# A seventh tile of columns in the first projection stage, with wider weight rows and one bank for two modulation sums

## The chip, the core and the metric

The kernel runs on one core of a Trainium2 chip. Five engines work beside one another: TensorE (PE in the profile; its weight loads are listed as PEld) multiplies matrices into PSUM, VectorE (DVE) and ScalarE (ACT) do elementwise work, GpSimd (POOL) clears a few tiles, and SyncE (SP) issues all DMAs, one after the other, in the order of its queue. The metric is the device time of one execution in microseconds.

## What is computed

One layer of a diffusion backbone: 256 latent tokens and 256 context tokens of width 2048. Everything starts with a modulated RMS norm and one wide projection; its columns feed an RWKV-7 branch (r, k, v, decay and rate inputs wd and ad, gate z), a latent-attention branch (q, kv, rope key, gate) and merge gates.

```python
def modulation(cond, w_mod, b_mod):
    m = (jax.nn.silu(cond) @ w_mod + b_mod).reshape(-1, 1, 3 * D_MODEL)
    return jnp.split(m, 3, axis=-1)

def project_stream(h, norm_w, shift, scale, w_in):
    hm = rmsnorm(h, norm_w) * (1 + scale) + shift
    return split_in(hm @ w_in)

...
        (rkv_x, zr_x, wd_x, ad_x, qd_x, kvd_x, kr_x, zm_x, mg_x) = project_stream(x, norm_w[i], sh_x, sc_x, w_in[i])
        (rkv_c, zr_c, wd_c, ad_c, qd_c, kvd_c, kr_c, zm_c, mg_c) = project_stream(ctx, norm_w[i], sh_c, sc_c, w_in[i])
...
        _, y_x = rwkv_scan(r_x, v_x, kk_x, dec_x, a_x, km_x, S_ctx)
...
        att_x = blocked_attend(q_x, jnp.concatenate([k_x, k_c], axis=1),
                               jnp.concatenate([v_x_att, v_c_att], axis=1))
        o_ml_x = att_x * jax.nn.silu(zm_x)

        x_new = x + g_x * merge_branches(o_rw_x, o_ml_x, mg_x, w_branch_rwkv[i], w_branch_mla[i], w_out[i])
```

The columns at issue are `kvd`, the 256 inputs of the keys and values of attention. They are needed for both streams, so a tile of 128 of these columns is 512 tokens wide.

## The kernel before

**Number format.** A product in full precision is three matmuls of rounded halves (`mm3`, line 234): high by high, high by low, low by high. A weight piece is loaded, cast to its high half on ACT (`wh`) and its low half is formed on DVE (`wl`); both are in `split` and `parts_of`, and profile lines show them as line 122, since a helper records every elementwise operation; matmuls show line 103, transposes line 107. The tiles are told apart by their names.

**First stage** (lines 256 to 389). The tokens `xT` lie transposed in 16 blocks of 128 rows, k = 0 to 15. For each k the modulation needs shift and scale of 128 channels: `mod_a(k)` loads four 512 KB pieces `wm` of the modulation's weights (11 buffers), multiplies them by `ssil`, the SiLU of the conditions, into a PSUM bank `pm` (32 matmul instructions), and copies the partial sums to `part`. `mod_b(k)` transposes `part` into the other half of the same bank and adds up on DVE, which gives `mod`. `scale_x`, two ACT operations and a split then make the modulated block, `hmh[:, k]` and `hml[:, k]`. `first(k, half)` multiplies it by the weights `w_first[k]`, 768 columns in two pieces of 384, three tiles of 128 columns per half, and adds into six accumulators `a0` to `a5` of 512 tokens. These are wd, ad, and k and v of the first two pairs of heads.

The loop of line 357 is written out as a software pipeline, and PE, ACT and DVE keep the order of the code: in turn k stand the modulated block k, `first(k-1, 0)`, `mod_a(k+1)`, `scale_x(k+1)`, the splits of the weights of k, `first(k-1, 1)`, `mod_b(k+1)`. SP's order is the planner's: the trace shows w_first(k), then the four wm of k+1. The two pieces of `w_first` take buffers of the general weight tag `w`, of which there are four; a `wl` of a half has two buffers, so its next one waits for `first` of the turn before.

Ahead of the loop stand the sums of squares of `xT`, `mod_a(0)`, `mod_b(0)`, the reciprocal root `rms`, and a matmul with the diagonal `dg` that spreads it over the partitions (`pst`, copied to `rsb`). On SP the order is vectors, constants, `xT` (4 MB in four), `cond`, then weights.

**PSUM** has eight banks in four tags of two: `acc`, `wk`, `lv`, `ch`. In the first stage the six accumulators hold `acc`, `wk`, `lv`, and the `pm` of even and odd k hold `ch`. Later `ch` carries the state updates of the scan (`chp`), `acc` the projections, `wk` the small work of the chains.

**Behind it.** Behind the first stage three things run together: a front chain that prepares heads, a back chain that scans them, and a background of projection tiles, `bg`. A background tile (`proj_g`) is 48 matmuls of 256 tokens, or of 512 where both streams are needed, with four weight pieces of 256 KB; it is taken in steps between the steps of the chains, and a clock of modelled engine times decides while tracing how many steps go where. The background takes what the chains need first (`main`), else the next of `extra`: the two kv tiles, 24 merge gates, the rope key, four q tiles, eight attention gates, eight merge gates. `kv_g(i)` projects tile 76 + i and spills it to DRAM, with sums of squares (`spill`). During attention the background gets a fixed number of steps per round (line 1401); what is left, the last merge gates and 16 tiles of the first branch's output (`branch_g`), runs in a row at line 1420, and then come the second branch and the output projection.

Of the kernel before, what the change touches and what calls it, by code (L numbers as in the profile page):

```python
# [9 lines left out]
F32 = mybir.dt.float32  # L10
# [3 lines left out]
ALU = mybir.AluOpType  # L14
AX = mybir.AxisListType

P = 128
D = 2048
KT = D // P
T = 256  # L20
TT = 2 * T
# [105 lines left out]
def hybrid_block(  # L127
# [20 lines left out]
    nc = tc.nc  # L148
# [65 lines left out]
    def piece(src, shape, pool=None):  # L214

        w = (pool or place[0]).tile(shape, F32, name="w", tag="w", bufs=NWU if pool else place[1])
        nc.sync.dma_start(w, src)
        return w

    def parts_of(w, pool=None, ns=None):  # L220

        h = (pool or place[0]).tile(list(w.shape), F32R, name="wh", tag="wh", bufs=ns or place[2])
        l = (pool or place[0]).tile(list(w.shape), F32R, name="wl", tag="wl", bufs=ns or place[3])
        with tc.high_priority(HP):
            split(w, h, l)
        return h, l
# [27 lines left out]
    lrl = cvp.tile([P, 2, TT], F32R, name="lrl", bufs=1)  # L254
    pp = ctx.enter_context(tc.tile_pool(name="pp", bufs=2, space=PSUM))
    with tc.tile_pool(name="p1", bufs=2) as p1:
        xT = p1.tile([P, KT, TT], F32, name="xT", bufs=1)
        for q in range(4):
            nc.sync.dma_start(xT[:, 4 * q:4 * q + 4], xcT[:, 4 * q:4 * q + 4])

        cv2 = p1.tile([P, 32], F32, name="cv2", bufs=1)
        nc.sync.dma_start(cv2, cond)
        st = p1.tile([P, 32], F32, name="st", bufs=1)
        S.activation(st, cv2, AF.Tanh, scale=0.5)
        V.scalar_tensor_tensor(st, st, 1.0, cv2, ALU.add, ALU.mult)
        V.memset(ssil, 0.0)
        V.tensor_scalar(ssil[:, 0:2 * KT], st, 0.5, None, ALU.mult)

        parts, mods = {}, {}

        def load_mod(k):
            for r in range(4):
                wm = p1.tile([P, 4, 256], F32, name="wm", tag="wm", bufs=NWM)
                nc.sync.dma_start(wm, w_mod_ss[k][:, 4 * r:4 * r + 4])
                yield wm

        def mod_a(k):

            pm = pp.tile([P, 512], F32, name="pm", tag="ch")
            for r, wm in enumerate(load_mod(k)):  # L280
                for g in range(4):
                    k0 = 2 * (4 * r + g)
                    E.matmul(pm[32 * g:32 * g + 32, 0:256], lhsT=ssil[:, k0:k0 + 32], rhs=wm[:, g],
                             start=r == 0, stop=r == 3, tile_position=(0, 32 * g))
            part = p1.tile([P, 256], F32, name="part", tag="part")
            S.copy(part, pm[:, 0:256])
            parts[k] = pm, part

        def mod_b(k):

            pm, part = parts.pop(k)
            for i in range(2):
                E.transpose(pm[:, 256 + 128 * i:384 + 128 * i], part[:, 128 * i:128 * i + 128], ident)
            mod = p1.tile([P, 4], F32, name="mod", tag="mod", bufs=4)
            for i in range(2):
                V.tensor_reduce(mod[:, 2 * i:2 * i + 2],
                                pm[:, 256 + 128 * i:384 + 128 * i].rearrange("p (g c) -> p c g", c=32)[:, 0:2], AX.X, ALU.add)
            V.tensor_scalar(mod[:, 0:2], mod[:, 0:2], vec("bsh", k), None, ALU.add)
            V.tensor_scalar(mod[:, 2:4], mod[:, 2:4], vec("bsc", k), 1.0, ALU.add, ALU.add)
            V.tensor_scalar(mod[:, 2:4], mod[:, 2:4], vec("norm", k), None, ALU.mult)  # L300
            mods[k] = mod


        pst = pp.tile([P, TT], F32, name="pst", tag="wk")
        for k in range(KT):
            sq = p1.tile([P, TT], F32, name="sq", tag="sq", bufs=4)
            if k % 2:
                S.activation(sq, xT[:, k], AF.Square)
            else:
                V.tensor_tensor(sq, xT[:, k], xT[:, k], ALU.mult)  # L310
            g = k % 4
            E.matmul(pst[32 * g:32 * g + 32], lhsT=con("ones")[:, 0:32], rhs=sq, start=k < 4, stop=k >= KT - 4,
                     tile_position=(0, 32 * g))
        sqs = p1.tile([P, TT], F32, name="sqs", tag="sq", bufs=4)
        S.copy(sqs, pst)
        pst = pp.tile([P, TT], F32, name="pst", tag="wk")
        for i in range(4):
            E.matmul(pst[:, 2 * i:2 * i + 2], lhsT=sqs[:, 128 * i:128 * i + 128], rhs=con("ones")[:, 0:2], start=True, stop=True)
        mod_a(0)
        mod_b(0)  # L320
        ms = p1.tile([P, 8], F32, name="ms", bufs=1)
        V.tensor_scalar(ms, pst[:, 0:8], 1.0 / (32 * D), 1e-6, ALU.mult, ALU.add)
        rms = p1.tile([P, 8], F32, name="rms", bufs=1)
        rsqrt(p1, rms, ms, 8)
        pst = pp.tile([P, TT], F32, name="pst", tag="lv")
        dg = p1.tile([P, 4, P], F32, name="dg", bufs=1)
        V.tensor_tensor(dg, ident.unsqueeze(1).to_broadcast([P, 4, P]), rms[:, 0:8:2].unsqueeze(2).to_broadcast([P, 4, P]), ALU.mult)
        E.matmul(pst, lhsT=con("ones"), rhs=dg.rearrange("p i t -> p (i t)"), start=True, stop=True)
        rsb = p1.tile([P, TT], F32, name="rsb", bufs=1)
        S.copy(rsb, pst)  # L330

        acc = [pp.tile([P, TT], F32, name=f"a{i}", tag=("acc", "wk", "lv")[i // 2]) for i in range(6)]
        wks = {}

        def first(k, half):
            wh, wl = wks[k][half]
            for i in range(3 * half, 3 * half + 3):
                cs = slice(128 * (i % 3), 128 * (i % 3) + 128)
                mm3(acc[i], wh[:, cs], wl[:, cs], hmh[:, k], hml[:, k], k == 0, k == KT - 1)

        hxs, ws = {}, {}

        def load_first(k):
            ws[k] = [piece(w_first[k][:, 384 * i:384 * i + 384], [P, 384]) for i in range(2)]

        def split_first(k):
            wks[k] = [parts_of(w) for w in ws.pop(k)]

        def scale_x(k):
            hxs[k] = p1.tile([P, TT], F32, name="hx", tag="hx")  # L350
            V.tensor_tensor(hxs[k], xT[:, k], rsb, ALU.mult)

        with tc.manual_schedule(engines={mybir.EngineType.PE, mybir.EngineType.Activation, mybir.EngineType.DVE}):
            scale_x(0)
            for k in range(KT + 1):
                if k < KT:
                    load_first(k)
                    mod, hx = mods.pop(k), hxs.pop(k)  # L360
                    for i in range(2):
                        t0 = slice(T * i, T * i + T)
                        S.activation(hx[:, t0], hx[:, t0], AF.Identity, scale=mod[:, 2 + i:3 + i], bias=mod[:, i:i + 1])
                    split(hx, hmh[:, k], hml[:, k])
                if k > 0:
                    first(k - 1, 0)
                if k + 1 < KT:
                    mod_a(k + 1)
                    scale_x(k + 1)
                if k < KT:  # L370
                    split_first(k)
                if k > 0:
                    first(k - 1, 1)
                if k + 1 < KT:
                    mod_b(k + 1)
        wd = p1.tile([P, TT], F32, name="sq", tag="sq", bufs=4)
        S.activation(wd, acc[0], AF.Tanh)
        split(wd, lrh[:, 0], lrl[:, 0])
        split(acc[1], lrh[:, 1], lrl[:, 1])

        def conv_kv(p, k, v):
            ck = cvp.tile([P, TT], F32, name="ck", tag="ck")
            conv(ck, k, "ck", p, 2)
            cv = cvp.tile([P, TT], F32, name="cv", tag="cv")
            conv(cv, v, "cv", p, 2)
            ckv[p] = (ck, cv)

        conv_kv(0, *acc[2:4])
        conv_kv(1, *acc[4:6])
# [96 lines left out]
        V.tensor_copy(sqd[:, col:col + 4], pss[:, 0:4])  # L486

    def kv_g(i):
        ps = yield from proj_g(76 + i, TT)
        for j in range(2):  # L490
            yield from spill(kvd[:, i, T * j:T * j + T], ps[:, T * j:T * j + T], 8 * i + 4 * j)

# [1012 lines left out]
def _layout(i):  # L1505
# [36 lines left out]
    wr, wk, wv = w[:, :1024], w[:, 1024:2048], w[:, 2048:3072]  # L1542
    wzr, wwd, wad, wqd = w[:, o[1]:o[2]], w[:, o[2]:o[3]], w[:, o[3]:o[4]], w[:, o[4]:o[5]]
    wkv, wkr, wzm, wmg = w[:, o[5]:o[6]], w[:, o[6]:o[7]], w[:, o[7]:o[8]], w[:, o[8]:o[9]]
    first = np.concatenate([wwd, wad, wk[:, :128], wv[:, :128], wk[:, 128:256], wv[:, 128:256]], 1)
    a["w_first"] = ca(first.reshape(KT, P, 768))
    allp = np.concatenate([wr, wzr, wzm, wk, wv, wmg, wqd, wkv], 1)
    nt = allp.shape[1] // P
    a["w_proj"] = ca(allp.reshape(2, 8, P, nt, P).transpose(3, 0, 2, 1, 4).reshape(nt, 2, P, 1024))
# [35 lines left out]
```

## Time and profile before

| | us |
|---|---|
| runs before: 1301.01, 1299.57, 1303.21; median | 1301.01 |
| profiled execution, first to last instruction (span) | 1295.7 |
| median less span | 5.3 |
| last matmul of the first stage ends, about | 135.7 |
| last branch store of the scan issued (orwd) | 912.7 |
| drain of the background starts | 1090.0 |

The list of runs has no time of its own for the profiled execution; its span is the time against which sums are made. In the views, a group is named by line, engine, operation and out<-in; a bracket at the end of a line gives the idle time of the engine before it and what ended it. The chain that ended last is followed back from the last instruction, at each step to what released it or to the one before it on its engine.

### The profile page before, as it was taken

What the parts mean: (1) busy time and instruction counts of PE and PEld (TensorE: products, weight loads), DVE (VectorE), ACT (ScalarE), POOL (GpSimd) and SP (SyncE); (2) the same over time, 40 slices, a digit from 0 to 9 for tenths busy, and PEclk for the clock granted to TensorE, in tenths of its full rate; (3) what the DMA queues carried; (4) which work ended last, traced back from release to release, by engine and by line L of the source; (5) the groups of instructions that cost most, each with busy time, mean ns of one, the idle gap of its engine ahead of it and who ended that gap; (6) DMA issues with size and microseconds to landing.
All of it is one profiled execution on the core that took longest, in us unless ns stands there. A gap on an engine that the chain in (4) does not pass through costs nothing.

```text
span 1295.7 us, 30060 instructions
## 1 busy us (share of the span) xinstructions
PE 1238.3 (96%) x11484; PEld 1040.8 (80%) x11484; DVE 949.4 (73%) x2658; ACT 571.1 (44%) x1183; POOL 3.3 (0%) x9
## 2 busy tenths in 40 slices
PE   5999989999999999999999998999999999999998
PEld 2666878788878778877788887878888889999887
DVE  4444876868797788788978886866877777569655
ACT  3343542442443433524524344343566655445443
POOL 0000000000000000000000000000000000000000
PEclk9999999989999999999999999999999999999999
DMA  9998445544453434533533445432853325988684
GB/s 375 356 358 308 126 136 143 140 127 113 107 143 100 118 97 121 141 79 104 154 99 103 113 121 131 114 97 88 247 169 113 102 59 168 309 273 278 214 264 140
DMA packets 172319, 212.09 MB, mean 164 GB/s; under 512 B 68560, under 2 KB 96848, under 8 KB 171664
## 3 DMA queue, kind: packets, MB, share of 16 engines
q1 hardware_dynamic: 172176, 210.18, 53.3%
q8 instruction: 90, 1.47, 0.5%
q14 instruction: 53, 0.43, 0.1%
HBM read 195.30 MB, written 14.82 MB: 162 GB/s over the span
## 4 chain that ended last, share of the span: by engine, by line
PE 66%; DVE 15%; DMA 13%; ACT 3%; issue 2%; SPq 1%; DVEq 0%; ACTq 0%
PE acc L103 31%; PE chp L103 11%; PE lv L103 9%; PE wk L103 6%; DMA w<-in_w_proj 5%; DMA wm<-in_w_mod_ss 4%; PE a L103 4%; DVE wl L122 4%; PE ch L103 3%; DVE BK L122 2%; PE wk L107 2%; ACT wh L122 1%; DVE wt L122 1%; PE pm L103 1%; DMA xT<-in_xcT 1%
## 5 line engine op out<-in xcount | busy, mean ns | idle before, releaser
L122 ACT CAST wh<-w 128x512 fp32r<-128x512 f32 (+1 forms) x484 | 291.4, 607 | 360.3 <-PE acc L103 144.2
L122 DVE TENSOR_TENSOR wl<-w,wh 128x512 fp32r<-128x512 f32 (+1 forms) x480 | 322.4, 675 | 146.9 <-ACT wh L122 89.4
L103 PE MATMUL acc<-hmh,wh 128*128 128x256 f32 (+1 forms) x1328 | 422.8, 319 | 4.4 <-ACT wh L122 4.2
L103 PE MATMUL acc<-hmh,wl 128*128 128x256 f32 (+1 forms) x1312 | 402.1, 307 | 4.9 <-DVE wl L122 4.7
L103 PE MATMUL acc<-hml,wh 128*128 128x256 f32 (+2 forms) x1328 | 406.1, 306 | 0.0
L103 PEld LDWEIGHTS acc<-hmh,wh 128*128 128x128 f32 x1328 | 252.2, 190 | 30.2 <-issue 7.4
L103 PEld LDWEIGHTS acc<-hmh,wl 128*128 128x128 f32 x1312 | 248.9, 190 | 22.1 <-DVE wl L122 8.3
L103 PEld LDWEIGHTS acc<-hml,wh 128*128 128x128 f32 (+1 forms) x1328 | 251.6, 189 | 11.4 <-issue 0.7
L122 DVE TENSOR_TENSOR pr<-wt 64x14 f32<-64x14 f32 (+6 forms) x224 | 42.6, 190 | 2.8
L122 DVE TENSOR_TENSOR wt<-wt,pr 64x14 f32<-64x14 f32 (+6 forms) x224 | 42.2, 189 | 2.3
L103 PE MATMUL a<-hmh,wh 128*128 128x512 f32 x96 | 40.7, 424 | 0.0
L122 DVE TENSOR_TENSOR W<-WT,lv 128x512 f32<-128x512 f32 x48 | 32.9, 685 | 9.8 <-PE lv L103 9.3
L103 PE MATMUL pm<-wm,ssil 128*32 128x256 f32 x512 | 34.9, 385 | 4.8 <-DMA wm<-in_w_mod_ss 4.5
L103 PE MATMUL a<-hmh,wl 128*128 128x512 f32 x96 | 37.9, 395 | 0.4 <-DVE wl L122 0.4
L103 PE MATMUL a<-hml,wh 128*128 128x512 f32 x96 | 37.9, 395 | 0.0
L103 PE MATMUL chp<-obh,wh 128*128 128x256 f32 x128 | 36.2, 283 | 0.0
L103 PE MATMUL chp<-obl,wh 128*128 128x256 f32 x128 | 36.2, 283 | 0.0
L103 PE MATMUL chp<-obh,wl 128*128 128x256 f32 x128 | 36.2, 283 | 0.0
L103 PEld LDWEIGHTS lv<-W,Z 64*64 64x64 f32 x1024 | 31.3, 135 | 3.6 <-issue 1.2
L122 ACT ACTIVATE hx<-hx,mod 128x256 f32<-128x256 f32 x32 | 17.5, 594 | 37.8 <-DVE mod L122 37.8
L122 DVE TENSOR_TENSOR AQ<-wk,cc 128x256 f32<-128x256 f32 (+1 forms) x48 | 24.4, 509 | 13.1 <-PE wk L103 12.7
L103 PE MATMUL lv<-W,Z 64*64 64x64 f32 x1024 | 33.8, 220 | 0.0
(314 smaller groups left out, 2107.6 us busy)
## 6 DMA issues: line engine op xcount, KB each, us to landing
w<-in_w_proj SPq DMA_DIRECT2D x296, 256.0 KB, 3.1
wm<-in_w_mod_ss SPq DMA_DIRECT2D x64, 512.0 KB, 7.5
w<-in_w_mod_g SPq DMA_DIRECT2D x64, 256.0 KB, 3.5
w<-in_w_br SPq DMA_DIRECT2D x64, 256.0 KB, 4.1
w<-in_w_out SPq DMA_DIRECT2D x64, 256.0 KB, 3.3
w<-in_w_first SPq DMA_DIRECT2D x32, 192.0 KB, 5.0
thd<-th SPq DMA_DIRECT2D x48, 128.0 KB, 3.5
xT<-in_xcT SPq DMA_DIRECT2D x4, 1024.0 KB, 8.5
```

The lines of the kernel that those rows point to most:

```text
L103: return self.engine.matmul(out, lhsT=lhsT, rhs=rhs, **kw)
L107: return self.engine.transpose(*a)
L122: return fn(out, *a, **kw)
```

## The change

- `cond` is loaded ahead of `xT`.
- One PSUM tile `pmm` in `ch` is allocated for the whole stage. The modulation of even k uses its first 256 columns, that of odd k the second 256; the transposes of `mod_b` go into the columns that `mod_a` had used for the same k.
- `mod_b(0)` is moved behind the matmul with `dg`.
- The freed `ch` bank holds a seventh accumulator `a6`: the first 128 columns of kv.
- `w_first[k]` has 896 columns, loaded in one DMA with rows of 3.5 KB into a tag `wf` of its own with two buffers, and split as 512 + 384 columns. `first` takes four tiles in its first half and three in its second.
- `kv_g(0)` no longer projects; it spills `a6`.

```diff
     with tc.tile_pool(name="p1", bufs=2) as p1:
+        cv2 = p1.tile([P, 32], F32, name="cv2", bufs=1)
+        nc.sync.dma_start(cv2, cond)
         xT = p1.tile([P, KT, TT], F32, name="xT", bufs=1)
...
-        cv2 = p1.tile([P, 32], F32, name="cv2", bufs=1)
-        nc.sync.dma_start(cv2, cond)
...
+        pmm = pp.tile([P, 512], F32, name="pm", tag="ch")
...
-            pm = pp.tile([P, 512], F32, name="pm", tag="ch")
+            pm = pmm[:, 256 * (k % 2):256 * (k % 2) + 256]
...
-                    E.matmul(pm[32 * g:32 * g + 32, 0:256], lhsT=ssil[:, k0:k0 + 32], rhs=wm[:, g],
+                    E.matmul(pm[32 * g:32 * g + 32], lhsT=ssil[:, k0:k0 + 32], rhs=wm[:, g],
...
-                E.transpose(pm[:, 256 + 128 * i:384 + 128 * i], part[:, 128 * i:128 * i + 128], ident)
+                E.transpose(pm[:, 128 * i:128 * i + 128], part[:, 128 * i:128 * i + 128], ident)
...
         mod_a(0)
-        mod_b(0)
...
+        mod_b(0)
         S.copy(rsb, pst)
 
-        acc = [pp.tile([P, TT], F32, name=f"a{i}", tag=("acc", "wk", "lv")[i // 2]) for i in range(6)]
+        acc = [pp.tile([P, TT], F32, name=f"a{i}", tag=("acc", "wk", "lv", "ch")[i // 2]) for i in range(7)]
...
-            for i in range(3 * half, 3 * half + 3):
-                cs = slice(128 * (i % 3), 128 * (i % 3) + 128)
+            for i in range(4 * half, 4 + 3 * half):
+                cs = slice(128 * (i % 4), 128 * (i % 4) + 128)
...
-            ws[k] = [piece(w_first[k][:, 384 * i:384 * i + 384], [P, 384]) for i in range(2)]
+            ws[k] = p1.tile([P, 896], F32, name="wf", tag="wf", bufs=2)
+            nc.sync.dma_start(ws[k], w_first[k])
...
-            wks[k] = [parts_of(w) for w in ws.pop(k)]
+            w = ws.pop(k)
+            wks[k] = [parts_of(w[:, 0:512]), parts_of(w[:, 512:896])]
...
-        ps = yield from proj_g(76 + i, TT)
+        ps = (yield from proj_g(77, TT)) if i else acc[6]
...
-    first = np.concatenate([wwd, wad, wk[:, :128], wv[:, :128], wk[:, 128:256], wv[:, 128:256]], 1)
-    a["w_first"] = ca(first.reshape(KT, P, 768))
+    first = np.concatenate([wwd, wad, wk[:, :128], wv[:, :128], wk[:, 128:256], wv[:, 128:256], wkv[:, :128]], 1)
+    a["w_first"] = ca(first.reshape(KT, P, 896))
```

## What the change does to the time: the prediction

> **What bounds the kernel now.** First the page: its head, the engines' totals and the 40 slices.
>
> ```profile
> span 1295.7 us, 30060 instructions
> PE 1238.3 (96%) x11484; PEld 1040.8 (80%) x11484; DVE 949.4 (73%) x2658; ACT 571.1 (44%) x1183; POOL 3.3 (0%) x9
> ...
> DMA  9998445544453434533533445432853325988684
> GB/s 375 356 358 308 126 136 143 140 127 113 107 143 100 118 97 121 141 79 104 154 99 103 113 121 131 114 97 88 247 169 113 102 59 168 309 273 278 214 264 140
> ```
>
> TensorE (PE) is busy nearly everywhere, but in the first four slices of 32.4 us the DMA engines are full as well. That is the first stage, the one that is edited. So the second view is the table of stretches, and the third the chain that ended last, cut to the first stage.
>
> ```profile
> 28.00:34.00 6.00, 4.71 (x39) 2.28 (x42) 3.75 (x11) 2.30 (x5) 0.00 (x0) 1.00 1.03 399
> 34.35:124.71 90.36, 86.64 (x680) 55.82 (x676) 40.44 (x117) 37.85 (x78) 0.00 (x0) 1.00 0.97 353
> ...
> 33.78 0.64 PE pm L103 x8
> 34.41 2.30 PE a L103 x9
> 36.93 2.10 PE a L103 x9
> 39.02 1.86 PE pm L103 x32
> 40.89 2.30 PE a L103 x9
> 43.41 2.10 PE a L103 x9
> 45.51 1.93 PE pm L103 x32
> ...
> 115.81 8.29 DMA wm<-in_w_mod_ss
> 124.14 0.64 PE pm L103 x8
> 124.78 2.30 PE a L103 x9
> 127.30 8.41 PE a L103 x36
> ```
>
> (Stretches: length, busy time of PE, weight loads, DVE, ACT, POOL, then granted clock, DMA share, GB/s.) One turn of the stage handles one k: 18 matmuls into the a tiles, 32 small ones into pm, two transposes. Where PE waits for nothing, a turn takes 45.51 - 39.02 = 6.49 us. But 13 turns lie between the two pm groups at 33.78 and 124.14, 6.95 us each: DMA sets the pace at share 0.97, and PE loses 13 x 0.46 = 6.0 us. After the last wm the stage is PE alone: 45 matmuls from 124.78 to 135.71, the last 36 at 8.41 / 36 = 0.2336 us.
>
> What lies behind it runs on PE with a background of projection tiles, and its end is found in the chain from 1090 us on and in the loads of the two weights there.
>
> ```profile
> 1089.98 67.87 PE acc L103 x580
> 1157.85 46.08 PE chp L103 x384
> ...
> L217 SPq DMA_DIRECT2D w<-in_w_proj x296: 323/328/1525, 131.5 to 1098.1; - x148
> ```
>
> The background is still unfinished when attention ends: 580 matmuls without a gap, 67.87 / 580 = 0.117 us each, drain what is left. So a background tile that no longer has to be run shortens this drain, whatever is done with the place it had.
>
> **The seventh tile, removed side.** kv tile 76 is 48 matmuls of 512 columns. They run now between 143.13 and about 158.4:
>
> ```profile
> 152.31 0.40 PE L103 MATMUL acc<-hml,wh 128*128 128x512 f32 x1
> ...
> 158.14 0.40 PE L103 MATMUL acc<-hmh,wl 128*128 128x512 f32 x1
> ```
>
> Between these two are 25 steps, 0.233 us each, so 48 cost 11.2 us. The background is taken in steps (three 512-wide matmuls, or six 256-wide ones of 0.117: 0.70 us both), so later tiles move up by 16 steps and the drain loses 96 matmuls of 0.117 us: **-11.2 us**. Its four weight loads, four casts and four differences go too:
>
> ```profile
> L122 ACT CAST wh<-w 128x512 fp32r<-128x512 f32 (+1 forms) x484 | 291.4, 607 | 360.3 <-PE acc L103 144.2
> L122 DVE TENSOR_TENSOR wl<-w,wh 128x512 fp32r<-128x512 f32 (+1 forms) x480 | 322.4, 675 | 146.9 <-ACT wh L122 89.4
> ```
>
> But up to attention it is replaced by two 256-wide tiles with eight splits: 4 x 0.675 = 2.7 us more DVE there. I charge 15% of it, DVE's share of the chain:
>
> ```profile
> PE 66%; DVE 15%; DMA 13%; ACT 3%; issue 2%; SPq 1%; DVEq 0%; ACTq 0%
> ```
>
> That is **+0.4 us**; its bounds are 0 and 2.7.
>
> **The same tile, added side.** Each turn gets three matmuls, 3 x 0.2336 = 0.70 us: PE's turn becomes 6.49 + 0.70 = 7.19. Data per turn go from 4 x 512 + 2 x 192 = 2432 KB to 2048 + 448 = 2496 KB.
>
> ```profile
> wm<-in_w_mod_ss SPq DMA_DIRECT2D x64, 512.0 KB, 7.5
> ...
> w<-in_w_first SPq DMA_DIRECT2D x32, 192.0 KB, 5.0
> ...
> cv<-in_cond SPq DMA_DIRECT2D x1, 16.0 KB, 11.2
> ```
>
> At the present rate of bytes that is 6.95 x 2496 / 2432 = 7.13 us; the rate may rise, since one load of 3.5 KB rows takes the place of two with 1.5 KB rows, half as many rows. The trace does not tell wm's rate from w_first's, so the DMA's turn (2496 KB are 2.556 MB) is bounded by 6.41, at the 399 GB/s of 28 to 34 us, and 7.24, at the 353 GB/s behind it; I take 7.13, which the 13 turns themselves give. All but the upper end lie under PE's 7.19: **the bound passes from DMA to PE**. Thirteen turns from 34.41 end at 34.41 + 13 x 7.19 = 127.9 instead of 124.78. Behind them stand 51 matmuls instead of 45: 10.93 + 6 x 0.2336 = 12.33. The stage ends at 140.2 instead of 135.71: **+4.5 us**. The two rates are so close that some turns will still wait; I add 0.4 (bounds 0, and 0.8 from 13 x (7.24 - 7.19) plus the last landing): **+4.9 us**. The wider split (512 + 384 columns instead of 2 x 384) costs DVE and ACT about 0.12 us a turn and hides: in the stretch above DVE is busy 40 of 90 us, ACT 38.
>
> **The shared bank.** If the two halves of one bank are held apart as a whole, pm's first matmul for k + 2 waits for the DVE sums of k + 1, where it had a bank of its own.
>
> ```profile
> 120.13 0.56 DVE L122 TENSOR_TENSOR wl<-w,wh 128x384 fp32r<-128x384 f32 x1 [0.94 <-PE a L103]
> 120.61 0.23 DVE L122 TENSOR_REDUCE mod<-pm 128x2 f32<-128x8 f32 x2
> ...
> 122.28 1.02 PEld L103 LDWEIGHTS pm<-wm,ssil 128*32 128x32 f32 x24 [0.36 <-issue]
> ```
>
> The sums end at 120.84, pm starts at 122.28: 1.44 us of room, 2.14 with the three new matmuls, which lie before it. Cost 0; behind a late sum all of PE would queue, and ACT's copy of the part behind that. The Trainium skill, "PSUM — Partial Sum Buffer", section "PSUM bank collisions raise a hardware error", asks for just this guard, by bank and quadrant and not by address. By it the wait exists; by these rows it has passed before anyone stands at it.
>
> **Head of the stage.** cond goes ahead of xT on SP, so xT is issued one DMA later:
>
> ```profile
> 3.64 0.46 SPq L262 DMA_DIRECT2D cv<-in_cond  x1
> ...
> 23.86 9.87 DMA wm<-in_w_mod_ss
> ```
>
> That is up to 0.46 us of delay for everything behind it, against a chain that from 23.86 waits for wm in any case; the earlier ssil and the later mod_b(0) (two transposes, five small DVE operations, behind the dg matmul) lie under that wait, since by 33.78 PE has caught up with wm. w_first(0) and (1) are 128 KB more in front of that landing (0.33 us at 399 GB/s), or nothing if long rows are cheaper. I take 0; bounds -0.5 and +0.8. On SP 16 issues fall away here and four later; wf's two buffers are two turns deep, as the four old pieces were. The seventh accumulator holds a ch bank until its spill, the second background task, some 150 us; the first chp matmul comes much later:
>
> ```profile
> L103 PEld LDWEIGHTS chp<-UV,AQ x512: 132/138/138, 209.2 to 897.1; 128*64 128x64 f32 x171
> ```
>
> Its two spills stand right behind the first projection now, their four small matmuls in banks that the front chain uses as well: 0 to +1, taken as 0.
>
> **Sum.** -11.2 + 0.4 + 4.9 = -5.9. Against the profiled execution the span goes from 1295.7 to 1289.8; the median of the runs is 1301.01, 5.3 more, which I take to lie around the span and to stay. **Forecast 1295.1 us.**
>
> **Rivals.** (1) *DMA keeps the first stage.* If the long rows bring nothing and the turn is at the upper 7.24 with waits in each, 13 x 0.05 + 1.2 more: 1297. For it: share 0.97 with every engine's queue already full; against: 399 GB/s before. The Trainium skill, "DMA: Bandwidth & Descriptors", section "Specifications", gives line rate from 512 B rows on and about 358 GB/s per core as HBM's limit, which speaks for this rival; the 399 GB/s above disagree for a short stretch.
> (2) *More is hidden.* The four splits leave the crowded start of the second stage, the first four of seven tiles are ready 2.1 us before the stage's end (three now), and the front chain starts earlier. Price: the 2.7 us of splits gained instead of 0.4 paid: 1292.
> (3) *The second stage's start loses its wide filler; slower.* A split feeds 12 matmuls: 2.80 us of PE when they are 512 wide, 1.40 when 256. With narrow tiles, 20 us of PE ask 14 splits, 9.6 us of DVE, instead of 4.8.
>
> ```profile
> 160.00:180.00 20.00, 20.00 (x132) 16.76 (x132) 11.59 (x37) 8.04 (x18) 0.00 (x0) 1.00 0.48 136
> 180.00:200.00 20.00, 15.36 (x111) 13.09 (x110) 15.90 (x49) 8.72 (x18) 0.00 (x0) 0.83 0.50 152
> ```
>
> 160 to 180 (wide) has a full PE and DVE at 11.6; 180 to 200 (narrow) has DVE at 15.9, PE idle for 4.6 us, and the clock at 0.83, another 0.17 x 20 = 3.4. Moved up, the narrow tiles bring the first row to 11.6 + 4.8 = 16.4, over the 15.9 where PE starved. A second such dip costs 8.0, and with the 2.7 us of splits in full in place of 0.4 it comes to -5.9 + 8.0 + 2.3 = +4.4: 1305.4. It decides from the point where DVE's share there passes that 0.8. Against: the second kv tile, wide too, moves up into just that place, and the dip at 180 falls in a burst of front work. (3b) Half of it: 1300.
> (4) *Nothing is hidden in the first stage*, because DMA's waits stay as long beside the added PE work: 48 x 0.2336 = 11.2 is paid in full, 11.2 comes back in the drain, and the 0.4 of splits is left: 1301.4.
>
> **How the numbers follow.** Forecast 0.50 (its own range 1292.5 to 1297.5, from the bounds of the head and the waits), (1) 0.13, (2) 0.10, (3b) 0.13, (3) 0.12, (4) 0.02. What a measurement can tell from no change is about 0.3%, 3.9 us. Faster, under 1297.1: 0.45 + 0.06 + 0.10 = 0.61. Within: 0.05 + 0.07 + 0.13 + 0.02 = 0.27. Slower, over 1304.9: 0.12. The range leaves out (3) and the lower part of (2): 1290.5 to 1302.5.
>
> **What would show it.** In the first stage: turns of 7.2 us without DMA waits at pm, the last a matmul near 140. DMA share below 0.97 there confirms that PE has taken over; turns of 7.3 and more with waits for wm are (1); a wait of pm for DVE's mod is the bank. In the drain, some 480 matmuls instead of 580. In the stretch 160 to 200, PE's idle time and clock tell (3). I am wrong if the drain is as long as before, or if it starts as many us later as it is shorter.

## The result, and the profile after

The changed kernel is slower. Its median is 1305.30 us (20 runs, 1301.22 to 1313.43), that of the kernel before in the same session 1299.81 us (20 runs, 1295.37 to 1306.56): a ratio of 1.0053, 95% interval 1.0039 to 1.0067, or +5.5 us where -5.9 was forecast. The profiled execution has a span of 1302.7 us against 1295.7.

The page of the changed kernel: head, engine totals, granted clock and DMA by slices of 32.6 us.

```profile
span 1302.7 us, 30013 instructions
...
PE 1243.6 (95%) x11484; PEld 1048.8 (81%) x11484; DVE 950.9 (73%) x2654; ACT 571.2 (44%) x1179; POOL 3.3 (0%) x9
...
PEclk8999999999999999999999999999999999998999
DMA  9999455443442343443433524433473323888684
```

PE has the same 11484 matmuls: the change moves work and removes none. The first slice of the clock is lower than the others, and so is one near the end. Those are two of three places that matter. The first is the head of the stage, in the timeline of PE and DVE of the changed kernel (start, duration, what, and in brackets the idle time before it):

```profile
9.34 1.29 DVE L122 TENSOR_TENSOR sq<-xT 128x512 f32<-128x512 f32 x2 [4.01 <-DMA xT<-in_xcT]
```
```profile
28.23 3.64 PE L103 MATMUL pm<-wm,ssil 128*32 128x256 f32 x32 [0.40 <-DVE mod L122]
...
32.88 0.50 PE L103 MATMUL a<-hmh,wh 128*128 128x512 f32 x1
...
36.14 1.93 PE L103 MATMUL pm<-wm,ssil 128*32 128x256 f32 x32
...
43.31 1.93 PE L103 MATMUL pm<-wm,ssil 128*32 128x256 f32 x32
```

The same two rows before the change, from the same views of the kernel before:

```profile
7.24 1.29 DVE L122 TENSOR_TENSOR sq<-xT 128x512 f32<-128x512 f32 x2 [4.03 <-DMA xT<-in_xcT]
```
```profile
L103 PE MATMUL a<-hmh,wh x96: 393/397/505, 28.2 to 134.8; 128*128 128x512 f32 x96
```
```profile
L103 PE MATMUL a<-hmh,wh x112: 393/397/503, 32.9 to 144.8; 128*128 128x512 f32 x112
```

(The second of these answers lists the matmuls of the accumulators: nanoseconds of one, then the start of the first and of the last; the line with x112 is the changed kernel's.) The squares of `xT` start 2.1 us later, and the first projection matmul 4.7 us later: 1.7 of the rest are 32 pm matmuls that take 3.64 us where a group takes 1.93 later on. The bracket in their row shows 0.40 more: they waited for DVE's sums `mod` of the k before, the sign that the prediction named for the shared bank. That wait comes once in the stage. From there on the stage behaves as forecast: a turn takes 43.31 - 36.14 = 7.17 us, and from the first to the last matmul it is 111.9 us where it was 106.6, so 48 matmuls, 11.2 us, were added for 5.3.

The stretches of the changed kernel show all three places (length, busy time of PE, weight loads, DVE, ACT, POOL, then clock, DMA share, GB/s):

```profile
28.00:34.00 6.00, 5.20 (x38) 2.24 (x39) 3.16 (x10) 3.01 (x6) 0.00 (x0) 0.64 0.82 325
36.00:124.00 88.00, 87.50 (x665) 59.19 (x668) 38.93 (x108) 36.73 (x73) 0.00 (x0) 1.00 0.96 348
160.00:180.00 20.00, 20.00 (x149) 17.09 (x149) 15.24 (x36) 8.64 (x21) 0.00 (x0) 1.00 0.43 131
180.00:200.00 20.00, 18.07 (x143) 16.09 (x142) 14.71 (x38) 10.48 (x23) 0.00 (x0) 0.91 0.62 183
733.00:765.00 32.00, 24.39 (x288) 19.13 (x287) 20.92 (x56) 9.84 (x21) 0.00 (x0) 0.95 0.44 69
1150.00:1180.00 30.00, 25.80 (x195) 25.45 (x194) 17.10 (x37) 11.36 (x20) 0.00 (x0) 0.89 0.89 303
```

The clock of 0.64 at 28 to 34 is the first place. The body of the stage has PE busy 87.5 of 88 us. The dip at 180 to 200, which rival (3) named, has become smaller (18.07 of 20 busy, 15.36 before). But PE idles 7.6 us at 733 to 765, and 4.2 us at 1150 to 1180, where it was busy 30.00 of 30 before.

The second place, in the waits of the changed kernel between 733 and 765, with the row of the store of g and of the loads of in_wup:

```profile
ACT wah L122 <- DMA th<-in_wup: 9.2, 1, 9.2
PEld acc L103 <- DVE wl L122: 5.4, 1, 5.4
PE acc L103 <- DVE wl L122: 5.0, 1, 5.0
```
```profile
L1431 SPq DMA_DIRECT2D gd<-gT x1: 432/432/432, 735.9 to 735.9; - x1
```
```profile
L688 SPq DMA_DIRECT2D th<-in_wup x8: 382/454/1330, 131.4 to 736.4; - x8
...
DMA to landing us min/median/max: 2.6/3.6/11.1
```

Line 1431 stores g transposed, 8 KB in pieces of 4 bytes. The load of in_wup right behind it is one of eight; their median is 3.6 us to landing, and one takes 11.1. ACT stands 9.2 us before its cast, and PE 5.0 us behind that. Before the change the store was issued at 780.5, when the last in_wup had been issued at 723.1. A load of w_proj was in flight with it then, and PE lost less, as two rows of the kernel before show, of its chain and of its waits from 776 to 812:

```profile
780.05 11.20 DMA w<-in_w_proj
```
```profile
PE acc L103 <- ACT wh L122: 2.0, 2, 1.5
```

The third place, in the chain that ended last of the changed kernel, behind the drain:

```profile
1103.04 44.75 PE acc L103 x379
...
1149.18 4.59 DMA thd<-th
...
1154.21 2.78 DMA thd<-th
...
1158.20 3.66 DMA w<-in_w_br
...
1163.53 4.79 DMA w<-in_w_br
...
1168.33 4.73 DMA gth<-thd
...
1173.72 26.31 PE chp L103 x197
```

The drain starts 13 us later than before, at 1103.0, and is shorter, as it should be: 464 matmuls. (The chain leaves it after 379 of them, and this view of it ends at 1200.) Its last matmul starts at 1157.5, before the change at 1157.6, so it ends where it had ended. But the loads for the second branch are not there when it ends. SP issues in order, and in its queue loads of `th` wait until one of four buffers has been stored (1149.18 and 1154.21); w_br and gth come behind them. Two rows of SP's own waits from 1085 to 1180, of the kernel before and of the changed one (us in total, times, longest), show that this wait is not new, but longer at a time:

```profile
SPq L1379 <- DMA thd<-th: 9.9, 12, 1.5
```
```profile
SPq L1382 <- DMA thd<-th: 15.2, 9, 2.8
```

How the lost time is counted: I cut the span into stretches of 5 us and add, for each, the time that PE wasn't busy and (1 - clock) x its busy time. Before: 64.3 us of 1295.7. After: 71.0 of 1302.7. What is left is 1231.4 and 1231.7, the same work, so the whole change of the span is lost time. (In the other versions with the same matmuls it is 1229.9 to 1233.6: such a sum is good to about 2 us.)

| PE's lost time, us | before | after |
|---|---|---|
| first stage (0 to 135; after: 0 to 145) | 18.6 | 18.7 |
| second stage and scan, up to the store of g (to 730; after: 700) | 28.0 | 23.5 |
| around the store of g (to 830; after: 760) | 7.9 | 10.0 |
| from there to the drain (to 1090; after: 1105) | 5.3 | 7.7 |
| drain and second branch (to 1200; after: 1205) | 0.0 | 6.7 |
| tail | 4.5 | 4.5 |

### The profile page after: what moved, and what is told of

It is laid out like the page before. It is cut to its first block, busy times and chain, and to the rows that moved or that the text cites. A ratio compares the mean times of both kernels' runs of the same rounds, so it can differ in the third digit from the quotient of the medians.

```text
span 1302.7 us, 30013 instructions
## 1 busy us (share of the span) xinstructions
PE 1243.6 (95%) x11484; PEld 1048.8 (81%) x11484; DVE 950.9 (73%) x2654; ACT 571.2 (44%) x1179; POOL 3.3 (0%) x9
## 5 line engine op out<-in xcount | busy, mean ns | idle before, releaser
L122 ACT CAST wh<-w 128x512 fp32r<-128x512 f32 (+1 forms) x448 | 273.7, 614 | 342.2 <-PE acc L103 144.1
L103 PE MATMUL acc<-hmh,wh 128*128 128x256 f32 (+1 forms) x1312 | 417.6, 318 | 5.1 <-ACT wh L122 5.1
L103 PE MATMUL acc<-hmh,wl 128*128 128x256 f32 (+1 forms) x1296 | 394.7, 305 | 7.9 <-DVE wl L122 7.8
L103 PE MATMUL acc<-hml,wh 128*128 128x256 f32 (+2 forms) x1312 | 400.2, 305 | 0.0
L122 DVE TENSOR_TENSOR wl<-w,wh 128x512 fp32r<-128x512 f32 (+1 forms) x444 | 301.5, 682 | 100.0 <-ACT wh L122 63.1
L103 PEld LDWEIGHTS acc<-hmh,wh 128*128 128x128 f32 x1312 | 248.5, 189 | 32.8 <-ACT wh L122 8.0
L103 PE MATMUL a<-hmh,wh 128*128 128x512 f32 x112 | 47.0, 420 | 0.1
L103 PE MATMUL a<-hmh,wl 128*128 128x512 f32 x112 | 44.4, 396 | 0.0
L103 PE MATMUL a<-hml,wh 128*128 128x512 f32 x112 | 44.2, 395 | 0.0
L122 DVE TENSOR_TENSOR wl<-wf,wh 128x512 fp32r<-128x512 f32 (+1 forms) x32 | 19.9, 625 | 32.7 <-ACT wh L122 21.9
```

Of the source, the lines that this page charges most:

```text
L103: return self.engine.matmul(out, lhsT=lhsT, rhs=rhs, **kw)
L122: return fn(out, *a, **kw)
```

## The experiments

Ratios are to the kernel before on the same chip; 1% is 13 us. The rows come from several chips, and a difference of two ratios carries the uncertainty of both.

| run | ratio | 95% interval |
|---|---|---|
| drop76 | 0.9923 | 0.9894 to 0.9953 |
| seventh_only | 1.0052 | 1.0031 to 1.0073 |
| cond_first | 1.0035 | 1.0015 to 1.0056 |
| bank_only | 0.9999 | 0.9978 to 1.0020 |
| a_th8 | 1.0022 | 1.0004 to 1.0040 |
| a_cond | 1.0017 | 0.9999 to 1.0034 |
| a_cond_th8 | 0.9985 | 0.9971 to 1.0000 |
| b_th8 | 0.9994 | 0.9978 to 1.0010 |
| a_all | 0.9906 | 0.9880 to 0.9933 |
| b_all | 0.9975 | 0.9956 to 0.9993 |
| s_cond_th8 | 1.0033 | 1.0014 to 1.0053 |
| cond_mid | 1.0002 | 0.9981 to 1.0023 |
| a_gdq | 0.9988 | 0.9970 to 1.0005 |
| b_gdq | 1.0014 | 0.9997 to 1.0031 |
| a_gd | 1.0000 | 0.9983 to 1.0017 |
| cond_act | 1.0010 | 0.9991 to 1.0030 |
| a_all2 | 0.9930 | 0.9907 to 0.9954 |
| a_th8_gd | 0.9957 | 0.9934 to 0.9980 |

### The parts of the change by themselves

**drop76**: the kernel before without the projection of tile 76. What is spilled in its place are constants, so this kernel leaves 48 matmuls out.

```diff
-        ps = yield from proj_g(76 + i, TT)
+        ps = (yield from proj_g(77, TT)) if i else cc[:, 0:TT]
```

> The kernel before with kv tile 76 not projected at all (its spill takes the constants; that part of the computation is left out). Theory A (the saved matmuls are worth their full PE time in the drain): 11.2 us less, ratio 0.9914, about 480 matmuls of acc in the drain, its start unmoved. Theory B (they were filler in the second stage, in time that PE would have lost anyway, or the order that follows loses more): ratio 0.996 or more, with the scan ending later or a new stall behind it.

-0.77%, 10.0 us (3.8 either way). The size is near the forecast's 11.2, but the place is another. The chain of this kernel still has a drain of 600 matmuls:

```profile
1079.81 70.76 PE acc L103 x600
```

It starts 10.2 us earlier than before (1089.98), so attention comes earlier and the drain isn't shorter. The last store of the scan is issued at 912.4 (912.7 before), the first load of it for what follows at 924.2 (930.3 before): six of the ten us lie between these two, where a loop takes background steps until the q tiles are done.

**seventh_only**: the changed kernel in which tile 76 is projected in the background as well, so 48 matmuls are run twice.

```diff
-        ps = (yield from proj_g(77, TT)) if i else acc[6]
+        ps = yield from proj_g(76 + i, TT)
```

> The changed kernel, but with tile 76 projected in the background as before, so the seventh tile's sum is made and not used. It shows the first stage's cost by itself. By the prediction +4.9 us (ratio 1.0038, last a matmul at 140.2); by the trace of the changed kernel the stage ends 9.9 us later (ratio 1.0076, last a matmul near 145.5). If later stages add losses of their own it is above that.

+0.52%, 6.8 us, with all that is new in the first stage: between the two sizes expected, 1.0038 and 1.0076. Nothing stalls behind its drain: no more than 0.1 us is lost from 1090 to 1205. With drop76's -10.0 the changed kernel should stand at -3.2; it stands at +5.5. The parts don't add up to the whole, so something arises only where both are there.

**bank_only**: the kernel before with the shared bank alone.

```diff
+        pmm = pp.tile([P, 512], F32, name="pm", tag="ch")
...
-            pm = pp.tile([P, 512], F32, name="pm", tag="ch")
+            pm = pmm[:, 256 * (k % 2):256 * (k % 2) + 256]
```

> The kernel before with the one bank for the sums of even and odd k, and nothing else; the second ch bank stays empty in the first stage. Theory H3 (the bank holds up the pipeline's start: pm of k=1 waits for the sums of k=0): first a matmul at 30 to 33 us instead of 28.2, wait of pm for DVE mod once, nothing in the later turns, stage end 0 to 3 us later. Rival (the bank costs in each turn): wait of pm for mod in most turns and the stage end 5 us or more later.

Nothing within 0.2%. Its trace has the one wait of pm for `mod` (0.4 us) that was expected, but the first projection matmul starts at 28.3 us, not at 30 or later. So the wait exists, once, and costs nothing that these runs can show.

### cond ahead of xT

**cond_first**: the kernel before with cond's load ahead of `xT`, nothing else.

> The kernel before with cond loaded ahead of xT, nothing else. Theory H1 (cond's short rows in front hold xT up): first square at about 9.3 us as in the changed kernel (7.24 before), but the time the same within 0.2%, since the stage waits for wm anyway. Theory H2 (xT was late by chance in that one profile): first square at 7.3 to 7.8 and no difference.

+0.35%: the expectation of no cost fell. First square at 9.55 us, first projection matmul at 30.6 (28.2 before).

**cond_mid**: the kernel before, cond's load between the second and the third quarter of `xT`.

```diff
         for q in range(4):
+            if q == 2:
+                nc.sync.dma_start(cv2, cond)
             nc.sync.dma_start(xT[:, 4 * q:4 * q + 4], xcT[:, 4 * q:4 * q + 4])
```

> The kernel before with cond's load between the second and the third quarter of xT. Theory (the 128-byte rows slow the loads that come behind them): first square at 7.2 to 7.5 us as before, the last quarter's squares some 2 us later than before (16.5 in place of 14.8), first projection matmul near 30, ratio 1.0015 to 1.0035. Rival (what counts is only that cond stands ahead of all of xT, at the start of the queues): first projection matmul at 28.5, ratio 1.000.

No cost. Its squares, from the timeline of DVE:

```profile
7.01 1.29 DVE L122 TENSOR_TENSOR sq<-xT 128x512 f32<-128x512 f32 x2 [3.85 <-DMA xT<-in_xcT]
...
14.69 1.29 DVE L122 TENSOR_TENSOR sq<-xT 128x512 f32<-128x512 f32 x2 [1.20 <-PE pst L103]
```

Neither the first nor the last quarter is late. My theory that the 128-byte rows slow what comes behind them is refuted; the rival holds. (The first projection matmul starts at 29.5 and not at 28.5: in this profile the `dg` matmuls took 2.08 us instead of 1.13, at a lower granted clock.)

**cond_act**: cond_first with the load issued from ACT's queue (`nc.scalar.dma_start` in place of `nc.sync.dma_start`).

> The kernel before with cond's load ahead of xT, issued from ACT's queue in place of SP's. Theory (the small rows delay xT only as the entries ahead of it in the same queue): first square at 7.2 to 7.6 us, ratio 1.000. Rival (what counts is that 128 small rows are carried at the start, whichever queue they are in): first square at 9 us or later, first projection matmul at 30 or later, ratio 1.002 to 1.005.

```profile
8.79 1.29 DVE L122 TENSOR_TENSOR sq<-xT 128x512 f32<-128x512 f32 x2 [5.12 <-DMA xT<-in_xcT]
```

The first square is 1.5 us late, a little short of the rival's 9 us, and the first projection matmul starts at 32.0: the place in SP's queue isn't it. The time, +0.10%, is below the rival's range, and its interval reaches from -0.09% to +0.30%, so what this place costs in the end is not settled by it.

In all seven profiles with cond ahead of all of `xT` the first square starts at 8.8 to 10.1 us, in all others at 6.9 to 7.6. So `xT` comes late when cond is issued ahead of all of it, whichever queue it takes, and not when two quarters stand in front. Why that is so is open.

### The stall behind the drain

**a_th8**: the changed kernel with eight buffers for `th` in the last stage. **b_th8**: the kernel before with the same edit.

```diff
-        return mg.tile([P, T], F32, name="th", tag="th", bufs=4)
+        return mg.tile([P, T], F32, name="th", tag="th", bufs=8)
```

> The changed kernel with eight th buffers in the last stage in place of four (the loads of th behind thd's stores no longer wait for one of the four to come free; the order of the matmuls and of the vector work is the same). Theory (the changed kernel's drain ends early and then waits for SP's queue, where a th load stands in front of w_br and gth): the PE gap at 1158 to 1174 us goes, 6.7 us of lost PE time between 1105 and 1205 become under 1, ratio to the kernel before 1.000 (0.998 to 1.002). Rival (the gap is the transfers' own time, not the buffers' order): gap stays, ratio 1.005.

> Control: the kernel before with eight th buffers. Theory (before, the drain's 600 matmuls cover the SP queue's waits, no lost PE time from 985 to 1200): ratio 1.000 (0.998 to 1.002). If the buffers help by themselves: ratio 0.995.

a_th8 stands 0.31% (4.0 us) lower than the changed kernel, just outside the range expected (0.998 to 1.002): of the 6.7 us lost in the trace, 4.0 come back in the time. b_th8 takes as long as the kernel before. (The 600 matmuls named for it are the drain of drop76; that of the kernel before has 580.) The gap is closed in the stretches of a_th8:

```profile
1150.00:1180.00 30.00, 30.00 (x256) 30.00 (x256) 21.75 (x43) 14.26 (x26) 0.00 (x0) 1.00 0.93 305
```

In its chain the drain is whole, and the second branch follows without a break:

```profile
1112.05 54.28 PE acc L103 x464
1166.33 46.08 PE chp L103 x384
```

The order of matmuls and vector work is that of the changed kernel, and SP's queue has no wait for `thd<-th` any more, so the buffers were the wait. 464 matmuls against 580 also confirm the forecast that the drain gets shorter.

**a_cond**: the changed kernel with cond behind `xT` again. **a_cond_th8**: both edits.

> The changed kernel with cond's load behind xT's again, nothing else. Theory (cond ahead of xT delays xT, and the delay is carried to the end): first square at 7.2 to 7.4 us in place of 9.34, first matmul of the first projection near 30.5 in place of 32.9, and the ratio 1.001 to 1.003 (2.3 to 4.6 us less than the changed kernel). Rival (the head's delay is absorbed by the DMAs of the stage, or comes from the placement of mod_b(0)): first projection matmul at 32 or later, ratio 1.005.

> Both edits of the two runs before together in the changed kernel. Theory (two separate losses, 2.3 to 4.6 us and 6.7 us): ratio 0.996 (0.994 to 0.999). Rival (the losses stand in for each other, or something further down takes the gain, such as the store of g in 4-byte pieces that holds the queue): ratio 1.000 to 1.002.

a_cond is 0.36% (4.7 us) under the changed kernel; its first square starts at 7.62 and the first projection matmul at 28.7. mod_b(0) is still moved in it, so that move shows no cost here. Both edits together give 0.68% (8.9 us), the sum of the two (0.67%): two losses apart from each other. But 0.9985 is -1.9 us, and not the forecast's -5.9.

**s_cond_th8**: a_cond_th8 with tile 76 projected a second time in the background.

> The changed kernel with cond behind xT and eight th buffers, in which tile 76 is projected a second time in the background (48 matmuls more than any other version). The difference to the run without them (ratio 0.9985) is what the 48 matmuls cost in the background; the difference to the kernel before is what the seventh tile costs in the first stage without cond's place. Theory: the stage costs 4.5 to 6 us (ratio 1.0035 to 1.0045), the matmuls 6.5 to 8 us. Rival (the head was not the reason that the seventh tile cost 6.8 us): ratio 1.005 or more.

The first stage by itself costs 0.33%, 4.3 us (interval 1.8 to 6.9; forecast 4.9). But the 48 matmuls are worth only 0.48%, 6.2 us, here (some 3 us either way), where 11.2 had been set down. So the lack is on the removed side.

### The store of g

**a_all**: a_cond_th8 with g turned on PE and stored as 16 rows. **b_all**: the kernel before with the same store and eight buffers. **a_gd**: the changed kernel with this store alone.

```diff
-    nc.sync.dma_start(gd.rearrange("c p -> p c"), gT)
+    pg = pp.tile([P, 512], F32, name="wk", tag="wk", bufs=2)
+    E.transpose(pg[0:KT, 0:P], gT, ident)
+    gr = mg.tile([KT, P], F32, name="gr", bufs=1)
+    S.copy(gr, pg[0:KT, 0:P])
+    nc.sync.dma_start(gd, gr)
```

> The changed kernel with cond behind xT, eight th buffers, and g stored as 16 rows of 512 bytes (gT transposed on PE and copied to SBUF first) in place of pieces of 4 bytes. Theory (all sites where the changed kernel loses PE time more than it must are closed: of the 10 us lost at 700 to 760, some 5 to 7 are the store of g, which holds the queue for 11 us): ratio 0.994 (0.992 to 0.997), PE's lost time between 700 and 760 at 3 to 5 us. Rival (that loss belongs to the start of the last stage and stays with a short store): ratio 0.998 to 0.999 as without this edit.

> The kernel before with eight th buffers and the same store of g in 16 rows. If the store of g costs both kernels alike: ratio 0.995 to 0.997, so that the move of the tile is worth 0.001 to 0.003 with everything else equal. If the kernel before hides it better: 1.000, and the move is worth 0.005.

> The changed kernel with the store of g in 16 rows alone (cond ahead of xT, four th buffers). Theory (the three losses add up: 10 us for this one as found with the other two closed): ratio 0.9975 (0.995 to 1.000). Rival (the loss is there only in the order of the other version): ratio 1.003 or more.

a_all is 0.79% (10.3 us) under a_cond_th8, more than the loss that I had seen there; b_all only 0.19% (2.5 us) under b_th8, which by itself is not clear of the noise (0.25%). PE's lost time from 700 to 770 falls from 13.4 us in a_cond_th8 to 3.3 in a_all. The changed kernel gains 6.9 us by this edit alone; its ratio of 1.0000 is the upper end of what was expected. In the trace of a_gd the wait for in_wup is gone:

```profile
L688 SPq DMA_DIRECT2D th<-in_wup x8: 383/452/1100, 129.3 to 736.2; - x8
...
DMA to landing us min/median/max: 2.5/3.3/6.0
```

The edit does two things: the rows are 512 bytes long, and the store is issued at 1157.8 instead of 735.9. Which of them counts isn't told apart; either way in_wup has no 4-byte pieces in front of it. The same 5 us of the changed kernel and of a_gd, in that order: with the pieces the DMA engines are 93% busy and move 34 GB/s, without them they are 27% busy and move 43.

```profile
740.00:745.00 5.00, 4.08 (x45) 3.00 (x43) 0.00 (x0) 0.00 (x0) 0.00 (x0) 1.00 0.93 34
```
```profile
740.00:745.00 5.00, 5.00 (x50) 3.93 (x49) 4.86 (x9) 3.82 (x9) 0.00 (x0) 1.00 0.27 43
```

**a_gdq**, **b_gdq**: a_cond_th8 and b_th8 with the store in 4-byte pieces as it was, from ACT's queue.

```diff
-    nc.sync.dma_start(gd.rearrange("c p -> p c"), gT)
+    nc.scalar.dma_start(gd.rearrange("c p -> p c"), gT)
```

> The changed kernel with cond behind xT and eight th buffers (ratio 0.9985 without more), with the store of g in its 4-byte pieces as it is, but issued from ACT's queue in place of SP's; the order of PE and DVE is the same. Theory (the store holds SP's queue for some 11 us, and the load of in_wup that stands right behind it comes late): ACT's wait for in_wup of 9.6 us goes, the lost PE time between 700 and 770 falls from 12 to 4 us, ratio 0.991 to 0.994. Rival (the pieces hold the 16 DMA engines whichever queue they are in): wait and ratio stay, 0.998 to 1.000.

> The kernel before with eight th buffers and the store of g from ACT's queue. Theory (behind the store stand loads that are needed less soon in the kernel before): 2 to 3 us gained, ratio 0.997 to 0.999. If the store costs both kernels alike: 0.993.

Neither gains (a_gdq 0.9988 beside 0.9985 without it; b_gdq, 1.0014 beside 0.9994, fits neither of its two expectations). In the waits of a_gdq, from 720 to 775, the wait is still 7.3 us, where a_cond_th8 has 9.6, though SP's queue is free of the store. The row behind it is that of ACT's queue, which carries nothing but this store, from the page of a_gdq (packets, MB, share of the span of 16 engines):

```profile
ACT wah L122 <- DMA th<-in_wup: 7.3, 1, 7.3
```
```profile
q10 hardware_dynamic: 2064, 0.01, 0.3%
```

So the order in SP's queue is at most the smaller part of it. The store alone, 0.01 MB, is 2064 packets (8 KB are 2048 pieces of 4 bytes), and 0.3% of 1299.7 us is some 4 us of all 16 engines, within the 11.2 us that it takes to land. My reading is that the pieces take the DMA engines from whoever needs them; that these 4 us make up the whole delay isn't shown. The Trainium skill, "DMA: Bandwidth & Descriptors", section "Issuing engines are not separate DMA queues", says that DMAs of all issuing engines run interleaved on the same 16 DMA engines, and this run agrees with it. A copy whose last dimension isn't contiguous becomes one descriptor for each element, by the section "Rules for kernel authors"; the trace counts packets and not descriptors, and has about one for each element.

### All three closed

**a_all2** is a_all once more; **a_th8_gd** is a_all with cond ahead of `xT` as in the change.

> The changed kernel with cond behind xT, eight th buffers and g stored in 16 rows, a second time on another chip (the first had only 6 runs, ratio 0.9906). Theory (the move of the tile gains once its three losses are closed): ratio 0.990 to 0.994. Rival (the first result was a fortunate chip): 0.995 to 0.998.

> The same kernel with cond ahead of xT, as the change has it: what cond's place alone costs where the other two losses are closed. Theory (the head's delay of about 2 us is carried to the end, with the cold clock behind it): 2 to 4.6 us over the run beside it, ratio 0.992 to 0.997. Rival (with the rest closed the delay is absorbed): within 1 us of the run beside it.

a_all2 gives 0.9930, a_th8_gd 0.9957: cond's place costs 0.27%, 3.5 us, also where the rest is closed. a_all2 stands 0.55% (7.2 us) under a_cond_th8, where a_all had 10.3. The version with the move of the tile and the three losses closed is the fastest of all that compute the whole layer, at 1286.9 us (6 runs) and 1289.4 us (8 runs) where the kernel before had 1299.1 and 1297.6. The same edits without the move give 0.9975. The move itself is worth 0.69% (9.0 us) beside a_all and 0.45% (5.8 us) beside a_all2, which ran on another chip than b_all. Both differences of two ratios are uncertain by about 0.3% (the two intervals, of 0.27% or 0.24% and 0.19%, put together).

## Why the prediction was wrong

The forecast was -5.9, the result +5.5: 11.4 us apart. The step that failed is "a background tile that no longer has to be run shortens this drain, whatever is done with the place it had", taken as 11.2 us of time. The drain did get shorter, but it started as many us later. The table of lost time says why: up to 1160 us PE had lost 59.8 us before and 59.9 after, with the same matmuls done, so the drain ends where it ended, and 6.7 us more are lost behind it. The forecast needed PE to lose 5.9 us less. The turns of the first stage and the second stage did lose less, but three things that the shift brings along, all set at nothing, took it back and more.

- **First stage, "the bound passes from DMA to PE": right.** A turn of 7.19 was forecast, 7.17 came (the 6.0 us that PE was said to lose before are in the length of the turns; as idle time the row has 3.7); +4.9 us for the stage, and s_cond_th8 has +4.3. The last matmul came some 5 us behind the forecast 140, nearly all of it from the head.
- **The shared bank at 0: right in the time** (bank_only), but not in "it has passed before anyone stands at it": at the head pm of the second k waits 0.40 us. The rows of that argument were taken from the end of the stage.
- **"Head of the stage ... I take 0; bounds -0.5 and +0.8": wrong.** I counted one issue of 0.46 us on SP and thought the chain covered it, since it waited for wm from 23.86 on. Instead `xT` landed 2.1 us later, and the first projection started later by that and more. Pairs with and without cond's place: 0.35 (cond_first), 0.36 (a_cond), 0.37 (a_th8 against a_cond_th8), 0.27% (a_th8_gd), 0.10% (cond_act): 3.5 to 4.8 us without the last.
- **"The drain loses 96 matmuls of 0.117 us: -11.2 us": the matmuls right, the time wrong.** The drain went from 580 matmuls to 464 (a_th8), some 480 being forecast. But I let the second branch start where the drain ends. A shorter drain leaves SP's queue less time for its `th` stores and loads, and w_br and gth came too late: 4.0 us (a_th8).
- **"So later tiles move up by 16 steps", at no cost beside the splits: wrong.** The gates end earlier too, and the store of g, in the trace at 735.9 instead of 780.5, falls just ahead of in_wup. That costs 6.9 us (a_gd) to 10.3 us (a_all), 2.5 of which the kernel before seems to pay as well (b_all, within the noise): 4.4 to 7.8 us more. The forecast had only asked what the tiles' splits do to DVE.

The three make 11.9 to 16.6 us (3.5 to 4.8, 4.0, 4.4 to 7.8), each difference of two ratios uncertain by some 3 us; that is enough for the 11.4. Where they come to more, a gain that the forecast had not counted fits: between the first stage and the store of g PE loses 23.5 us in place of 28.0 in the two profiles.

Of the rivals, (1) asked for a stage that DMA paces; PE was busy 87.5 of 88 us, so it falls. (3) had the sign and the size, 1305.4, by luck: the second dip that it asked for at 160 to 200 didn't come. That stretch lost 3.6 us where it had lost 7.3 (the rival's 8.0 counted the lower clock over all 20 us, not over PE's busy time), and the first 165 us behind the stage lost as much as before (15.6 and 15.3). The sentence "or if it starts as many us later as it is shorter" is what came: 13 us later, 13.6 us shorter (116 matmuls of 0.117). What I hadn't asked is why it could start late: because the work taken out of it had to run somewhere ahead, and ahead PE lost no less than before.

How much of a single profile is chance: the clock. a_cond_th8 and a_cond have the same code at the head; the first lost 4.4 us to a lower granted clock there, the second none. Of six profiles with this head (cond behind `xT`, `mod_b(0)` moved, one bank) two lost over 4 us, a_all2 the other; of the six with `mod_b(0)` in its old place and cond behind `xT` as before none lost more than 1.6. Whether the new order makes it likelier was not tested.

## What to carry to other kernels

Where PE is full nearly everywhere, moving work can win only what PE loses at the place to which the work goes, and everything behind shifts: look for each short transfer on the way, and ask in front of what it lands after the shift. A stage that gets shorter takes cover from the loads of the next one; count the buffers and the queue that bring these, not only the matmuls that go. A transfer that is put ahead of the first load that everybody waits for can delay it by more than its bytes would take, however small it is.

## What the runs showed of the hardware

- A load of 16 KB in rows of 128 bytes, issued ahead of a load of 4 MB at the start, makes that load's first quarter come some 2 us later (first square at 8.8 to 10.1 us in seven profiles, 6.9 to 7.6 in the others); between its quarters it costs nothing that cond_mid shows (1.0002). At 399 GB/s, the rate of 28 to 34 us, I estimate 0.04 us for its bytes.
- A store of 8 KB in pieces of 4 bytes is 2064 packets (a_gdq). With it in front, a load of 128 KB took 11.1 us to land where the median is 3.6, and 9.6 us when the store was issued from another queue (a_gdq).
- A dip of PE costs more than its idle time. The 32 pm matmuls behind the late start took 3.64 us instead of 1.93, with a clock of 0.64 in the stretch. In the 5 us stretches of the two kernels a dip is followed by 1.2 to 3.1 us of lost clock, or by none; at the head of a_cond_th8 it was 4.4. The Trainium skill, "TensorE: Matmul & The Clock Gate", section "What's actually happening", has the clock at half until the array has been busy for a window of about 3.4 us, from which I estimate 1.7 us. The sums of the two kernels lie around it, the 4.4 does not.
